# The last output product split around two rows' transposes, the root's table loaded early, the layer norm's transposes one product earlier

## The chip, the cores and the metric

The kernel runs on one core of a Trainium2 chip. The metric is the time of one execution on the device, in microseconds (us). The core has TensorE (PE, the matrix products), VectorE (DVE), ScalarE (ACT), GpSimd (POOL) and SyncE (SP); each works through its own instructions in order, and they wait for each other by semaphores. DMAs are issued here from SP and POOL, and one or two from ACT.

## The reference

One decoder layer on 512 tokens with a model width of 1024, in fp32. Three branches run beside each other, are weighed by gates and merged; an output product and a gated feed-forward part with a short convolution follow:

```python
h = rmsnorm(x) * norm_mix_g
p_a, p_b, q, p_g = split(h @ w_in, [3072, 5120, 6144])          # 9216 columns
gb, gc, v = split(p_a, 3);  y_a = (gb * causal_dwconv3(gc * v)) @ w_a_out
u, ug = split(p_b, 2);      u = causal_dwconv31(u * sigmoid(ug)) + bias
y_b = silu(layernorm(u)) @ w_b_out                              # "branch B"
y_c = attention(q, rmsnorm(mem) @ w_kv) @ w_att_out             # 4 heads, 256 memory tokens
g = sigmoid(p_g + b_gate)
x = x + (g[0] * y_a + g[1] * y_b + g[2] * y_c) @ w_o
u = causal_dwconv3(rmsnorm(x) @ w_up);  gt, up = split(u, 2)    # 2 x 2816 columns
x = x + (silu(gt) * up) @ w_down
return rmsnorm(x) * norm_final_g
```

## The kernel before, in words

**Arithmetic.** Each factor of a product is split into a high and a low part of a format that PE reads faster than fp32, and three matmuls (high by high, high by low, low by high) stand for one. For weights the high part is a copy on ACT (L481, `whi`) and the low part a difference on DVE (L485, `wlo`); activations are split in the same way. Large products are made of blocks by a scheme with seven products in place of eight: a *quad* has products numbered 1, 5, 2, 6, 7, 4, 3, whose operands are sums and differences of activation blocks (`b00`, `b10`, `b11`, `t4` to `t7`, the names in the profile's `fb10h`, `ft4h` and so on) and of weight blocks. Products are summed up in PSUM banks and read out between them: the read of one product frees the bank, or puts away a part result, before the next may go on. The reads of a quad are called r1 to r7; those on ACT are copies (L704 is r6, L712 is r4), those on DVE are additions or subtractions (L438 is r7). One quad product (L662) is 24 matmuls of 256 columns, 128 deep.

**Order.** PE's order is written out by hand. Everything else is a job with an engine, a cost, what must be done before it, and the buffers that it takes or uses. A small planner in the kernel works out from PE's order when each job is due, shifts some kinds of job by a table of constants, plays the engines forward with the jobs' costs, and writes down in which order each engine issues its jobs. The order of ACT, DVE, SP and POOL is therefore made anew when a job is added or PE's order changes. On the chip these orders are fixed: an instruction that waits holds up everything behind it on its engine.

**Around the first two edits' place (about 500 to 546 us).** The last two quads of the input projection are gates ("gate (1,0)" and "gate (1,1)"), with the small products of the merge among them. Meanwhile branch B's layer norm runs: a sum of squares on DVE, its sum over the columns on PE (`pe_squares`), the root on ACT (in `scale_jobs`), the reciprocal on DVE, and then `pe_rows`: four transposes on PE (L800) that spread the factor of each token over all partitions. After them DVE multiplies four blocks by these rows (L1318, `lns`), ACT applies the swish, and ACT and DVE make the operands of branch B's product (L1367, L1372 and others; Y in the planner's words). That product, `mq`, is two quads whose products alternate. The gates' sigmoids are L1492, on ACT. Both sigmoid and swish need a table of their own on ACT, and so does the square root; a change shows as ACT_TABLE_LOAD in the trace.

**Around the other edits' place (about 580 to 612 us).** The merged sum is multiplied by w_o in seven products a, b, f, c, d, e, g, each in two halves (`pe_wo(p, i)`, i the half of the inner dimension; L432 to L434; f alone in single fp32 matmuls). The results are added to or subtracted from x's rows on DVE (L1730, `add_row`). The rows are four blocks of 128 tokens, here called the first to the fourth row (t = 0 to 3); the first two are finished by the products up to e, the other two by g. For each row follow: the square with its sum on ACT (L1737), the root on ACT (L1743), reciprocal and scaling on DVE (L1747, L1748, `xnorm`), eight transposes on PE (L1756, `pe_transpose_rows`), and from the two transposed banks the high parts on ACT (L1768), the low parts on DVE (L1774) and plain copies on ACT (L1781, `h2b`), from which the operands of the up projection are made. The up projection's first products (b00, (up 0, 1) and on) need the first two rows, later ones the other two. Product g writes to banks that the adds of an earlier product must have read. In the kernel before, the first row's transposes stand ahead of g's first half and the second row's between its halves; the third's and fourth's follow in the up projection.

Of the kernel before, what the change touches and what calls it, by code (L numbers as in the profile page):

```python
# [17 lines left out]
SEQ = 512  # L18
NT = SEQ // P
# [297 lines left out]
def hybrid_block_kernel(  # L317
# [19 lines left out]
    nc = tc.nc  # L337
# [27 lines left out]
    job = jobs.add  # L365
# [28 lines left out]
    def dve(n):  # L394
        return (n + 151) / 960.0 - 0.08

    def actv(n):
        return (n + 224) / 1200.0 - 0.08
# [21 lines left out]
    def par(key, i):  # L420
        return pk[:, cols[key] + i : cols[key] + i + 1]
# [23 lines left out]
    def pe(key, cost, fn, after=(), take=(), use=(), unit=True):  # L445
        pe_jobs[key] = (cost, fn, after, take, use)
        seq.append(key)
        if unit:
            the_unit(key, key)

    def the_unit(unit, last):
        unit_at[unit] = len(unit_uses)
        unit_uses.append((unit, last))
# [282 lines left out]
    def column(i, n):  # L736
        return cols_1[:, i : i + n]

    R_MEM, R_X, R_V, SS_X, ATT = column(0, MC), column(2, NT), column(60, NT), 6, 12
# [46 lines left out]
    def squares_to_tokens(bank, key, n, width, total=1024):  # L786

        ps, sq = make(bank), tiles[key]
        for c in range(n):
            for j in range(0, total, width):  # L790
                nc.tensor.matmul(
                    ps[:, c : c + 1], sq[:, j + c * P : j + (c + 1) * P], mean_col,
                    start=j == 0, stop=j + width == total,
                )

    def along_tokens(bank, r, n):

        ps = make(bank)
        for c in range(n):
            nc.tensor.transpose(  # L800
                ps[:, c * P : (c + 1) * P], r[:, c : c + 1].broadcast_to([P, P]), ident
            )
# [205 lines left out]
    def pe_squares(s, key, n, width, after, total=1024):  # L1008
        pe((s, "squares"), n * (total // width) * 0.22,
           lambda: squares_to_tokens(("ss", s), key, n, width, total), after,  # L1010
           take=[(("ss", s), "ps")], use=[key], unit=False)

    def pe_rows(s, r, n):
        pe((s, "rows"), n * 0.11, lambda: along_tokens(("rows", s), r, n), [(s, "scale")],
           take=[(("rows", s), "ps")], unit=False)
# [419 lines left out]
    for p in range(4):  # L1435
# [5 lines left out]
            lambda k, j, p=p: par("conv_a_w", k * KC + 2 * p + j), [("CV", p), ("ldp",)], ANY,  # L1441
# [15 lines left out]
    def merge_product(br, m, g):  # L1457
        w_hi, w_lo = w_units.pop(("merge", br, m, g))
        for j in range(2):
            bank = ("bank", "y", br, m, j)  # L1460
            ps = make(bank) if g == 0 else tiles[bank]
            at = slice(j * P, (j + 1) * P)
            for i in range(4):
                k = 4 * g + i
                hi, lo = (two((s, k // 2))[:, k % 2, :] for s in PARTS[br])
                first, last = k == 0, k == KC - 1
                nc.tensor.matmul(ps, w_hi[:, i, at], hi, start=first, stop=False)  # L1467
                nc.tensor.matmul(ps, w_hi[:, i, at], lo, start=False, stop=False)  # L1468
                nc.tensor.matmul(ps, w_lo[:, i, at], hi, start=False, stop=last)  # L1469

    def pe_merge(br, m, gs=(0, 1)):
        banks = [("bank", "y", br, m, j) for j in range(2)]
        for g in gs:
            parts = [(s, 2 * g + i) for i in range(2) for s in PARTS[br]]
            ready = PARTS_READY[br]
            ready = ready[len(ready) // 2 * g : len(ready) // 2 * (g + 1)]
            pe(("merge", br, m, g), 24 * MM, lambda g=g: merge_product(br, m, g),
               [("wl", ("merge", br, m, g))] + ready,
               take=[(b, "ps") for b in banks] if g == 0 else [],
               use=parts + (banks if g else []))  # L1480

    for br in (2, 0, 1):
        for m in range(4):
# [27 lines left out]
            elif br == 1:  # L1511
# [23 lines left out]
                for r in range(2):  # L1535
                    part = ("mg", r, m // 2)

                    def merged(m=m, gate=gate, r=r, part=part):
                        if m % 2 == 0:
                            make(part)  # L1540
                        at = slice(r * HALF, (r + 1) * HALF)
                        nc.vector.tensor_tensor(
                            four(part)[:, 2 * (m % 2) : 2 * (m % 2) + 2, :],
                            two(("g", 2, m))[:, :, at], two(gate)[:, :, at], op=ALU.add,
                        )
# [45 lines left out]
    def wo_bank(p):  # L1591


        return "a" if p in "aceg" else "f" if p == "d" else p
# [77 lines left out]
    for n, p in enumerate(WO):  # L1672
        if p in "ab":
            m = 0 if p == "a" else 2
# [5 lines left out]
    def wo_lows(p, i):  # L1680
        return ("mgl", p, i) if p in "ab" else ("mgl", p)
# [24 lines left out]
    def pe_wo(p, i):  # L1706

        before = WO_BEFORE.get(p)
        for ts in ((0, 1),) if p in "ab" else ((0,), (1,)):
            banks = [("bank", "wo", wo_bank(p), t) for t in ts]  # L1710
            if p in WO_WHOLE:
                work, cost, needs = wo_whole, 2 * MM_WHOLE, [whole[p, i][1]] + merged(p)
                parts = [SPLIT_FROM[p], whole[p, i][0]]
            else:
                work, cost, needs = wo_product, 6 * MM, [("wl", ("wo", p, i)), wo_lows(p, i)]
                parts = [("mgh", p), ("mgl", p)]
            if i == 0 and before:
                needs += [("x1", before, t) for t in ts]
            new = p not in WO_BEFORE and i == 0
            key = ("wo", p, i) if len(ts) == 2 else ("wo", p, i, ts[0])  # L1720
            pe(key, cost * len(ts), lambda ts=ts: work(p, i, ts), needs,
               take=[(b, "ps") for b in banks] if new else [],
               use=parts + ([] if new else banks), unit=False)
        if (p, i) not in WO_HELD and p not in WO_WHOLE:
            the_unit(("wo", p, i), key)
# [9 lines left out]
    def row_square(t):  # L1735
# [2 lines left out]
            tiles["xnorm", t], tiles["x1", t], AF.Square, accum_out=column(SS_X + t, 1)  # L1738
        )

    def row_root(t):
        r = column(SS_X + t, 1)
        nc.scalar.activation(r, r, AF.Sqrt, bias=eps, scale=1.0 / D)  # L1743
# [48 lines left out]
    for t in range(NT):  # L1792
        both = [("x1", p, t % 2) for p in WO if any(r == t // 2 for r, _, _ in WO_READ[p])]
        job(("keep", t), "SP", 1.6, lambda t=t: nc.sync.dma_start(
            out=x1_kept[t], in_=tiles["x1", t]), both, LOAD_LATENCY, use=[("x1", t)])
        job(("xsquare", t), "ACT", actv(1024), lambda t=t: row_square(t), both,
            take=[(("xnorm", t), "sb")], use=[("x1", t)])
        job(("xroot", t), "ACT", 0.3, lambda t=t: row_root(t), [("xsquare", t)])
        job(("xnorm", t), "DVE", 1.40, lambda t=t: row_norm(t),
            [("xroot", t), "ldg"], use=[("xnorm", t), ("x1", t), ("gffn",)])  # L1800
        for i in range(2):
            bank, r = ("bank", "tr", t, i), t // 2
            if (i, r) != (0, 1):
                job(("rh", t, i), "ACT", actv(512), lambda t=t, i=i: row_high(t, i), [("tr", t)],
                    use=[bank])
                job(("rl", t, i), "DVE", dve(512), lambda t=t, i=i: row_low(t, i), [("rh", t, i)],
                    use=[bank])
                form_ready.setdefault(("h2", f"b{i}{r}"), []).append(("rl", t, i))
            blk = ("h2b", i, r)
            job(("rb", t, i), "ACT", actv(512), lambda t=t, i=i: row_block(t, i), [("tr", t)],  # L1810
                use=[bank] + ([blk] if t % 2 else []), take=[] if t % 2 else [(blk, "lf")])
            blocks_ready[i, r].append(("rb", t, i))

    def pe_transpose_rows(t):
        pe(("tr", t), 0.87, lambda: transpose_rows(t), [("xnorm", t)],
           take=[(("bank", "tr", t, i), "ps") for i in range(2)], use=[("xnorm", t)], unit=False)
# [55 lines left out]
    for do in (  # L1872
# [16 lines left out]
    GATE = {(br, i): ("gate", br, i) for br in range(3) for i in range(2)}  # L1889
# [19 lines left out]
        (GATE[0, 1], 3): lambda: [pe_merge(0, m) for m in range(3)],  # L1909
        (GATE[1, 0], 6): lambda: pe_mean("mu"),  # L1910
        (GATE[1, 1], 6): lambda: (
            pe_squares("v", ("csq", 0), NT, SEQ, [("var", "fold")], SEQ), pe_merge(0, 3, (0,))),
        (GATE[1, 1], 7): lambda: (pe_rows("v", R_V, NT), pe_merge(0, 3, (1,))),
        (GATE[1, 1], 3): lambda: [
            multiply_job(("mq", q), f, "y") for f in (1, 5, 2, 6, 7, 4, 3) for q in range(2)],
    }
# [3 lines left out]
            beside[q, f]()  # L1920

    for p in WO:
        for i in range(2):
            if p == "g":
                pe_transpose_rows(i)
            pe_wo(p, i)


    ENDS = [slice(0, 256), slice(256, 512)]
# [168 lines left out]
    for u, ps in enumerate(PAIR_UNITS):  # L2098
        n = ps.stop - ps.start
        for p in "abe":  # L2100
            i, j = {"a": (0, 0), "b": (1, 0), "e": (1, 1)}[p]
# [217 lines left out]
```

## Time and profile before

| | |
|---|---|
| median of 3 runs | 934.01 us (931.47 to 934.22) |
| the profiled execution | 931.92 us by its time, span 930.2 us from the first to the last instruction |
| mean granted PE clock in it | 0.996 of full speed |
| busy share | PE 98%, PE's weight loads 93%, DVE 91%, ACT 74%, POOL 15% |
| DMA | 196.91 MB, mean 212 GB/s |

How to read the rows that follow: in a row of the timeline the numbers are the start in us from the beginning of the span and the duration; then come engine, line of the kernel, operation, output <- inputs, shapes, and xN for N like instructions in a row. Square brackets give how long the engine stood idle just before, and for whom. In the view of waits a row gives the total, the number and the longest of such waits. In the table by stretches a row is a stretch of time, its length, the busy time of PE, weight loads, DVE, ACT and POOL with the instructions counted, and at the end the granted clock, the busy share of the DMA engines and GB/s.

### The profile page before, as it was taken

What the parts mean: (1) busy time and instruction counts of PE and PEld (TensorE: products, weight loads), DVE (VectorE), ACT (ScalarE), POOL (GpSimd) and SP (SyncE); (2) the same over time, 40 slices, a digit from 0 to 9 for tenths busy, and PEclk for the clock granted to TensorE, in tenths of its full rate; (3) what the DMA queues carried; (4) which work ended last, traced back from release to release, by engine and by line L of the source; (5) the groups of instructions that cost most, each with busy time, mean ns of one, the idle gap of its engine ahead of it and who ended that gap; (6) DMA issues with size and microseconds to landing.
All of it is one profiled execution on the core that took longest, in us unless ns stands there. A gap on an engine that the chain in (4) does not pass through costs nothing.

```text
span 930.2 us, 17118 instructions
## 1 busy us (share of the span) xinstructions
PE 915.1 (98%) x6813; PEld 863.5 (93%) x6813; DVE 848.1 (91%) x976; ACT 686.0 (74%) x938; POOL 137.4 (15%) x165
## 2 busy tenths in 40 slices
PE   9999999999999999999999999999999999999996
PEld 8999999999889999999899897799999999988885
DVE  7998999999989999999886999797999889999986
ACT  8577988889978867878767983686766667765665
POOL 0121111000011111120101211111221111002300
PEclk9999999999999999999999999999999999999999
DMA  9999579745688898887868899889999886689952
GB/s 363 382 251 227 123 182 220 166 114 113 165 183 222 204 203 202 215 187 212 181 140 214 199 252 330 206 211 305 278 245 230 201 167 128 169 313 316 248 110 91
DMA packets 55952, 196.91 MB, mean 212 GB/s; under 512 B 6336, under 2 KB 6464, under 8 KB 55872
## 3 DMA queue, kind: packets, MB, share of 16 engines
q0 software_dynamic: 22608, 81.54, 48.4%
q1 hardware_dynamic: 32544, 113.23, 33.5%
q8 instruction: 53, 0.87, 0.4%
q10 hardware_dynamic: 720, 1.06, 0.3%
q14 instruction: 27, 0.22, 0.1%
HBM read 191.60 MB, written 4.19 MB: 211 GB/s over the span
## 4 chain that ended last, share of the span: by engine, by line
PE 83%; issue 7%; DMA 4%; DVE 3%; ACT 1%; POOL 1%; ACTq 0%; POOLq 0%; DVEq 0%
PE bank L662 55%; PE bank L432 6%; PE bank L434 6%; PE bank L433 5%; PE bank L1469 3%; PE bank L1467 3%; PE bank L1468 3%; PE bank L918 2%; DMA wo<-in_w_o 2%; DMA wf<-in_w_b_out 2%; DMA wf<-in_w_up 1%; DVE wlo L485 1%; ACT whi L481 0%; PE bank L1155 0%; POOL whol L502 0%
## 5 line engine op out<-in xcount | busy, mean ns | idle before, releaser
L481 ACT CAST whi<-wf 128x1024 fp32r<-128x1024 f32 x202 | 210.6, 1045 | 92.4 <-PE bank L662 37.5
L485 DVE TENSOR_TENSOR wlo<-wf,whi 128x1024 fp32r<-128x1024 f32 (+1 forms) x196 | 235.8, 1210 | 23.5 <-ACT whi L481 23.2
L1227 ACT ACTIVATE tp<-u,pk 128x510 f32<-128x510 f32 (+22 forms) x184 | 119.0, 705 | 4.5 <-DVE acc L1234 2.0
L1234 DVE TENSOR_TENSOR acc<-acc,tp 128x988 f32<-128x988 f32 (+22 forms) x92 | 109.0, 1186 | 8.8 <-ACT tp L1227 7.4
L619 POOL DMA_DIRECT2D wf<-in_w_in x48 | 42.9, 908 | 230.7 <-DVE wlo L485 167.4
L662 PE MATMUL bank<-fb10h,whi 128*128 128x256 f32 x248 | 69.0, 278 | 1.7 <-ACT g L712 1.3
L662 PE MATMUL bank<-fb10l,whi 128*128 128x256 f32 x248 | 68.6, 277 | 0.6 <-DVE fb10l L1372 0.6
L662 PE MATMUL bank<-ft6h,whi 128*128 128x256 f32 x248 | 68.7, 277 | 0.1
L662 PE MATMUL bank<-fb11h,wlo 128*128 128x256 f32 x248 | 68.6, 277 | 0.1
L662 PE MATMUL bank<-ft6l,whi 128*128 128x256 f32 x248 | 68.7, 277 | 0.0
L662 PE MATMUL bank<-fb00h,whi 128*128 128x256 f32 x248 | 68.7, 277 | 0.0
L662 PE MATMUL bank<-ft5l,whi 128*128 128x256 f32 x248 | 68.7, 277 | 0.0
L662 PE MATMUL bank<-fb11h,whi 128*128 128x256 f32 x248 | 68.7, 277 | 0.0
L662 PE MATMUL bank<-ft7h,whi 128*128 128x256 f32 x248 | 68.7, 277 | 0.0
L662 PE MATMUL bank<-ft7l,whi 128*128 128x256 f32 x248 | 68.7, 277 | 0.0
L662 PE MATMUL bank<-ft7h,wlo 128*128 128x256 f32 x248 | 68.7, 277 | 0.0
L662 PE MATMUL bank<-fb00l,whi 128*128 128x256 f32 x248 | 68.6, 277 | 0.0
L662 PE MATMUL bank<-fb00h,wlo 128*128 128x256 f32 x248 | 68.6, 277 | 0.0
L662 PE MATMUL bank<-ft6h,wlo 128*128 128x256 f32 x248 | 68.6, 277 | 0.0
L662 PE MATMUL bank<-ft5h,wlo 128*128 128x256 f32 x248 | 68.6, 277 | 0.0
L662 PE MATMUL bank<-ft5h,whi 128*128 128x256 f32 x248 | 68.6, 277 | 0.0
L662 PE MATMUL bank<-fb11l,whi 128*128 128x256 f32 x248 | 68.5, 276 | 0.0
(416 smaller groups left out, 3151.7 us busy)
## 6 DMA issues: line engine op xcount, KB each, us to landing
wf<-in_w_in SPq DMA_DIRECT2D x52, 512.0 KB, 5.1
wf<-in_w_in POOLq DMA_DIRECT2D x48, 512.0 KB, 6.2
wf<-in_w_up POOLq DMA_DIRECT2D x31, 512.0 KB, 7.3
wf<-in_w_up SPq DMA_DIRECT2D x29, 512.0 KB, 7.9
wf<-in_w_down SPq DMA_DIRECT2D x15, 512.0 KB, 4.5
wf<-in_w_att_out SPq DMA_DIRECT2D x8, 512.0 KB, 3.8
wf<-in_w_a_out SPq DMA_DIRECT2D x8, 512.0 KB, 3.7
wf<-in_w_b_out SPq DMA_DIRECT2D x8, 512.0 KB, 6.4
```

The lines of the kernel that those rows point to most:

```text
L432: nc.tensor.matmul(ps, s_hi, w_hi, start=start, stop=False, skip_group_check=again)
L433: nc.tensor.matmul(ps, s_hi, w_lo, start=False, stop=False, skip_group_check=again)
L434: nc.tensor.matmul(ps, s_lo, w_hi, start=False, stop=stop, skip_group_check=again)
L481: nc.scalar.copy(parts[0], src())
L485: nc.vector.tensor_tensor(lo, src(), hi.bitcast(F32), op=ALU.subtract)
L619: nc.gpsimd.dma_start(out=tiles[key], in_=block(w, col[c], k), accum_op=ALU.add)
L662: nc.tensor.matmul(ps[:, c, :], w[:, k, at], a[k], start=first and n == 0, stop=i == 3 and n == 2, skip_group_check=again,)
L1227: nc.scalar.activation(two(("tp", p, s))[:, j, s:], two(("u", p))[:, j, : SEQ - s], AF.Copy, scale=weight(j),)
L1234: nc.vector.tensor_tensor(a, a, two(("tp", p, s))[:, :, s:], op=ALU.add)
L1467: nc.tensor.matmul(ps, w_hi[:, i, at], hi, start=first, stop=False)
L1468: nc.tensor.matmul(ps, w_hi[:, i, at], lo, start=False, stop=False)
L1469: nc.tensor.matmul(ps, w_lo[:, i, at], hi, start=False, stop=last)
```

## The change

Three things are changed. In the last of the output products, g, the order on PE was: first row's transposes, g's first half, second row's transposes, g's second half. It becomes: first half, both rows' transposes, second half. A job "roots" loads the square root's table on ACT by itself, after all twelve sigmoid jobs, and each root of the rows depends on it. And the four transposes of the layer norm's factors (`pe_rows("v", ...)`) move from behind product 7 of the gate quad (1,1) to a place ahead of it, behind half of a merge product.

```diff
@@ -1738,6 +1738,9 @@
             tiles["xnorm", t], tiles["x1", t], AF.Square, accum_out=column(SS_X + t, 1)
         )
 
+    job("roots", "ACT", 1.28, lambda: nc.scalar.preload_act_table_set("sqrt_and_others"),
+        [("sigmoid", br, m) for br in range(3) for m in range(4)])
+
     def row_root(t):
         r = column(SS_X + t, 1)
         nc.scalar.activation(r, r, AF.Sqrt, bias=eps, scale=1.0 / D)
@@ -1795,7 +1798,7 @@
             out=x1_kept[t], in_=tiles["x1", t]), both, LOAD_LATENCY, use=[("x1", t)])
         job(("xsquare", t), "ACT", actv(1024), lambda t=t: row_square(t), both,
             take=[(("xnorm", t), "sb")], use=[("x1", t)])
-        job(("xroot", t), "ACT", 0.3, lambda t=t: row_root(t), [("xsquare", t)])
+        job(("xroot", t), "ACT", 0.3, lambda t=t: row_root(t), [("xsquare", t), "roots"])
         job(("xnorm", t), "DVE", 1.40, lambda t=t: row_norm(t),
             [("xroot", t), "ldg"], use=[("xnorm", t), ("x1", t), ("gffn",)])
         for i in range(2):
@@ -1909,8 +1912,9 @@
         (GATE[0, 1], 3): lambda: [pe_merge(0, m) for m in range(3)],
         (GATE[1, 0], 6): lambda: pe_mean("mu"),
         (GATE[1, 1], 6): lambda: (
-            pe_squares("v", ("csq", 0), NT, SEQ, [("var", "fold")], SEQ), pe_merge(0, 3, (0,))),
-        (GATE[1, 1], 7): lambda: (pe_rows("v", R_V, NT), pe_merge(0, 3, (1,))),
+            pe_squares("v", ("csq", 0), NT, SEQ, [("var", "fold")], SEQ), pe_merge(0, 3, (0,)),
+            pe_rows("v", R_V, NT)),
+        (GATE[1, 1], 7): lambda: pe_merge(0, 3, (1,)),
         (GATE[1, 1], 3): lambda: [
             multiply_job(("mq", q), f, "y") for f in (1, 5, 2, 6, 7, 4, 3) for q in range(2)],
     }
@@ -1920,10 +1924,11 @@
             beside[q, f]()
 
     for p in WO:
-        for i in range(2):
-            if p == "g":
-                pe_transpose_rows(i)
-            pe_wo(p, i)
+        pe_wo(p, 0)
+        if p == "g":
+            for t in range(2):
+                pe_transpose_rows(t)
+        pe_wo(p, 1)
 
 
     ENDS = [slice(0, 256), slice(256, 512)]
```

## The prediction

> **What bounds the kernel now.** First the page's busy times, then who TensorE (PE) waited for, then the granted clock in the stretches where it waited.
>
> ```profile
> PE 915.1 (98%) x6813; PEld 863.5 (93%) x6813; DVE 848.1 (91%) x976; ACT 686.0 (74%) x938; POOL 137.4 (15%) x165
> ```
>
> PE is busy for 915.1 of 930.2 us, and the change removes no product. So it can only win or lose in PE's waits and in stretches where PE runs slowly. The view of waits, for PE alone, names them (us in total, times, longest):
>
> ```profile
> PE bank L662 <- ACT g L712: 1.3, 1, 1.3
> PE bank L1756 <- DVE cols L1747: 1.0, 1, 1.0
> PE bank L662 <- DVE y L438: 1.0, 1, 1.0
> PE bank L432 <- DVE x L1730: 0.8, 1, 0.8
> PE bank L662 <- DVE fb10l L1372: 0.6, 1, 0.6
> PE bank L662 <- ACT fb10h L1367: 0.5, 1, 0.5
> ```
>
> The change touches both places these come from: four waits (L662) lie in the last branch's product at 526 to 546 us, two (L1756, L432) before and after the first transpose of the normed rows. The table by stretches (length; busy us by engine; then the granted clock, DMA share and GB/s) adds a third loss:
>
> ```profile
> 529.80:533.20 3.40, 2.14 (x19) 1.94 (x18) 3.40 (x5) 3.38 (x5) 0.86 (x1) 1.00 0.95 387
> 591.70:595.10 3.40, 1.53 (x11) 0.99 (x10) 3.36 (x5) 3.40 (x5) 0.00 (x0) 1.00 1.04 271
> 595.10:598.50 3.40, 3.40 (x9) 2.63 (x10) 3.40 (x4) 1.25 (x3) 0.00 (x0) 0.50 0.06 13
> ```
>
> After the two waits around the transpose PE runs 3.4 us at half clock, which costs 1.7 us. After the 1.3 us wait in the first row the clock stays at 1.00. So in reach are 1.9 us of waits and 1.7 us of slow clock at 592 to 598, and 3.3 us of waits at 526 to 546.
>
> **Part A: the layer norm's transposes one product earlier.** Moving four transposes ahead of a 2.8 us product costs PE nothing in itself, and the scaling by the norm (L1318) can start 2.4 us sooner (a product less the transposes). But both queues behind it are written in an order that a planner makes, and it comes out anew. Comparing the two programs' orders, one thing matters: on ScalarE (ACT) the read L712, which frees the PSUM bank for the second b10 product, now has ahead of it all that it had before, and two things more: the second half of t4's high part, and one more change of table, because the sigmoids and swishes alternate once more before it.
>
> ```profile
> 532.23 1.28 ACT L1492 ACT_TABLE_LOAD   x1
> 533.52 1.34 ACT L1492 ACTIVATE g<-g,pk 128x512 f32<-128x512 f32 x2
> ...
> 537.70 0.40 ACT L1367 CAST ft4h<-acc 128x256 fp32r<-128x256 f32 x1
> 538.01 0.40 ACT L1367 CAST ft4x<-acc 128x256 fp32r<-128x256 f32 x1
> 538.31 0.57 ACT L704 COPY y<-bank 128x512 f32<-128x512 f32 x1
> ```
>
> Counted from start to start (neighbouring rows overlap by 0.1 us), the load takes 1.29 us and the two casts 0.61, so L712 comes 1.90 us later, because ACT has no gap there to take them in. The earlier norm does not help it: ACT, not the norm, is late. What PE does with that:
>
> ```profile
> 529.78 0.28 PE L662 MATMUL bank<-fb10h,wlo 128*128 128x256 f32 x1
> 531.32 0.38 PE L662 MATMUL bank<-fb10h,whi 128*128 128x256 f32 x1 [1.26 <-ACT g L712]
> ...
> 546.18 0.39 PE L662 MATMUL bank<-ft4h,whi 128*128 128x256 f32 x1 [0.99 <-DVE y L438]
> ```
>
> The product at 531.32 moves to 533.22. The two waits before it (0.5 and 0.6) go, since swish and b10's parts now come before L712; PE then only arrives earlier and stands in one piece for 0.46 + 0.56 + 1.26 + 1.90 = 4.2 us. The later wait of 0.99 is for VectorE's (DVE) subtraction L438, which is not moved by L712: PE comes 1.90 later and waits 0.99 less. Part A costs 1.90 - 0.99 = **0.9 us**. Bounds: nothing if ACT were to gain what the norm gains, 1.9 if L438 is late by as much.
>
> A page of the Trainium skill, ScalarE: Activation LUTs (What ACT_TABLE_LOAD costs), puts a change of set at about 2.66 us, load and drain. Here the next activation starts 1.29 us after the load does, so the trace does not agree and decides; by that figure part A would cost, as an estimate, 1.4 us more.
>
> **Part B: the root's table and the last output product.** The table now loads before the output product, just ahead of a read (L704) whose product has time to spare: after it ACT has this gap.
>
> ```profile
> 542.40 1.05 ACT L481 CAST whi<-wf 128x1024 fp32r<-128x1024 f32 x1 [1.07 <-PE bank L662]
> ```
>
> There I take it as free; without that cover it would cost up to 1.28 us. What it leaves, at 590 us, is on the path:
>
> ```profile
> 586.66 1.05 ACT L481 CAST whi<-wo 128x1024 fp32r<-128x1024 f32 x1 [2.84 <-PE bank L434]
> 587.62 1.05 ACT L1737 ACTIVATE xnorm<-x 128x1024 f32<-128x1024 f32 x1
> 588.57 0.18 ACT L1737 ACTIVATION_READ_ACCUMULATOR xnorm<-x 128x1 f32 x1
> 588.66 1.04 ACT L1737 ACTIVATE xnorm<-x 128x1024 f32<-128x1024 f32 x1
> 589.61 0.18 ACT L1737 ACTIVATION_READ_ACCUMULATOR xnorm<-x 128x1 f32 x1
> 589.81 1.28 ACT L1743 ACT_TABLE_LOAD   x1
> 591.11 0.48 ACT L1743 ACTIVATE cols<-cols,eps 128x1 f32<-128x1 f32 x2
> ```
>
> ```profile
> 593.03 1.28 DVE L1748 SCALAR_TENSOR_TENSOR xnorm<-x,cols,gffn 128x1024 f32<-128x1024 f32 x1
> 594.23 1.28 DVE L1730 TENSOR_TENSOR x<-x,bank 128x512 f32<-128x512 f32 x2
> ```
>
> ```profile
> 591.64 0.39 PE L434 MATMUL bank<-whi,mgl 128*128 128x512 f32 x1
> 593.06 1.06 PE L1756 MATMUL bank<-ident,xnorm 128*128 128x128 f32 x8 [1.03 <-DVE cols L1747]
> 594.96 0.67 PE L432 MATMUL bank<-whi,mgh 128*128 128x512 f32 x1 [0.84 <-DVE x L1730]
> ...
> 599.42 1.04 PE L1756 MATMUL bank<-ident,xnorm 128*128 128x128 f32 x8
> 600.21 0.48 PE L432 MATMUL bank<-whi,mgh 128*128 128x512 f32 x1
> ...
> 603.02 0.28 PE L662 MATMUL bank<-fb00h,whi 128*128 128x256 f32 x1
> ```
>
> Product e ends at 592.03 (593.06 - 1.03). Product g needs the adds L1730, which in both programs stand on DVE behind both normed rows. So g must wait for the whole chain in either order; new is only that the transposes no longer stand between. The squares are pinned by the weights that arrive at 586.6, so without the load the chain is 1.30 us earlier: adds at 592.93, g at 593.66. By part A e ends 0.9 later, at 592.96: PE stands 0.7 us. Then a half of g (600.21 to 603.02: 2.81), both rows' transposes (0.79 each, 599.42 to 600.21), the other half: 593.66 + 2.81 + 1.58 + 2.81 = 600.86, against 603.02. That is **-2.2 us**, part A's 0.9 counted in, if the clock holds.
>
> **Part C: what the bunched transposes make late.** After them ACT has four casts and four copies in one go, ahead of the next row's square; in the trace they come in two groups, the first under the slow product. On DVE the difference for (up 0, 5) now stands ahead of the third row's norm, which it did not.
>
> ```profile
> 599.62 1.05 ACT L481 CAST whi<-wf 128x1024 fp32r<-128x1024 f32 x1 [3.26 <-PE bank L434]
> 600.57 0.58 ACT L1768 CAST fb00h<-bank 128x512 fp32r<-128x512 f32 x1
> ...
> 604.67 1.06 ACT L1737 ACTIVATE xnorm<-x 128x1024 f32<-128x1024 f32 x1 [0.39 <-DVE x L1730]
> ```
>
> ```profile
> 602.16 0.69 DVE L1774 TENSOR_TENSOR fb00l<-bank,fb00h 128x512 fp32r<-128x512 f32 x1 [0.24 <-ACT h2b L1781]
> ...
> 604.56 1.22 DVE L485 TENSOR_TENSOR wlo<-wf,whi 128x1024 fp32r<-128x1024 f32 x1
> ...
> 606.48 1.29 DVE L1748 SCALAR_TENSOR_TENSOR xnorm<-x,cols,gffn 128x1024 f32<-128x1024 f32 x1
> ```
>
> The 0.24 shows that the readers of one transposed bank on ACT and DVE wait for each other; in the new order it is the copies that wait for the differences. From the end of g's first half: 0.2 until its result is out, a high part 0.97, four casts 2.0 (3.2 so far); meanwhile DVE does a difference of 1.14 and four of 0.60, the third done at 4.3; the last three copies follow it (5.9), a high part (6.9), the square and its sum (7.9), the high part of (up 0, 5) (8.9), its difference on DVE (10.1), reciprocal and norm (11.6). PE has until then 1.58 + 2.81 and two products of 2.83 (603.02 to 605.85, and up to 608.68), 10.05. So it waits **1.6 us** for the third row; in the trace it does not wait there. Bounds: 1.0 if the copies don't wait for the differences, 1.9 if the (up 0, 5) weights are late.
>
> **The sum.** The profiled execution took 931.92 us by its time, with a span of 930.2. Without a fall of the clock: -2.2 + 1.6 = -0.6, so 931.3. Does it fall? In the trace it fell when no product ran from 592.03 to 594.96, 2.9 us, and did not after 1.26. Part A's gap is 4.2 us, longer than the one that lost the clock; B's is 0.7, C's 1.6 with 0.79 of transposes behind it. So I expect one fall, in A: 1.7 us. Part of that comes back. PE then ends e at 594.66; the second square waits for d's add and g starts at about 595.0, 1.34 later than without the fall and not 1.7. So +0.8 instead of -0.6: 932.7.
>
> The runs' median, 934.01, lies 2.1 above the profiled execution, and the trace doesn't show why (another fall would be 1.7). I put half of it, 1.0, on the forecast: **933.7 us**, -0.3 against the median, +1.8 against the profiled one. That is no change, as 0.3% (2.8 us) is about what a measurement of this kernel can tell.
>
> **Rivals.** *The clock holds in A.* The third loss goes entirely: 931.3, or 932.3 with the 1.0. For it: 1.26 us and then 0.99 us of waiting left the clock at 1.00. Against it: the gap is three times as long. The Trainium skill, TensorE: Matmul & The Clock Gate (Part 1: The HAM clock gate), has the clock halve after at least one idle window of some 3.4 us, free-running. Taken strictly, a 4.2 us gap holds a whole window in about one case of four, an estimate from its figure, and this rival would be the likeliest; the trace, where a gap of 2.9 us with transposes in it was enough, doesn't agree with so strict a reading, and I weigh it a little below the forecast.
>
> *The clock falls again in C* (slower): with the transposes PE has no product for 1.6 + 0.79 = 2.4 us there, near the 2.9 that lost it. Then 1.7 more, paid in full: 934.4 in the frame of the profiled execution, 936.5 with the full 2.1, and with the upper ends of A and C (1.0 and 0.3) 937.8. It decides from a gap of about 2.4 us on.
>
> *The change doesn't do what it says in A*: if L712 is not delayed, because ACT gains the norm's lead, A gains up to 0.9 and the gap stays under 2.9: about 930.4, or 931.4 with the 1.0.
>
> **Numbers.** Chances: forecast 0.42, clock holds 0.25, a second fall 0.23, A not as said 0.10. Faster by over 0.3% means below 931.2: a third of the clock that holds (0.08) and seven tenths of the last (0.07), 0.15. Slower means above 936.8: two thirds of the second fall (0.15) and a fifth of the forecast, its upper ends (0.08), 0.23. Within: 0.62. The range goes from 930.4 (A not as said, in the frame of the profiled execution) to 937.8 (the second fall with its upper ends), and little of either case lies outside.
>
> **What would show it.** Of the profile after: one PE wait of about 4 us for L712 in place of three, no wait for L438; at g one wait of about 0.7 for L1730 and none at L1756 there; a wait of 1 to 2 us at the third row's transposes (L1756). No table load between squares and roots. One stretch of half clock behind the first of these, none at 595. Wrong would be: no wait at the third row, a long wait for L712 missing, or table loads in a new place that PE waits for.

## The result, and the profile after

The changed kernel takes 935.13 us (median of 14 runs, 933.71 to 935.80), the kernel before 931.88 (14 runs, 931.04 to 934.22). The ratio, estimated over all these runs, is 1.0030 with a 95% interval of 1.0023 to 1.0037, that is 2.8 us; the medians lie 3.25 us apart. The profiled execution of the changed kernel took 934.44 us with a span of 932.7, against 931.92 and 930.2: 2.5 us.

The page's busy times and the view of waits for PE, kernel after (L1759 and L1750 are L1756 and L1747 of the kernel before):

```profile
PE 916.5 (98%) x6813; PEld 866.2 (93%) x6813; DVE 848.9 (91%) x976; ACT 686.5 (74%) x938; POOL 137.1 (15%) x165
```

```profile
PE bank L662 <- ACT g L712: 4.6, 1, 4.6
...
PE bank L1759 <- DVE cols L1750: 1.3, 1, 1.3
PE bank L432 <- DVE x L1730: 0.7, 1, 0.7
```

The three short waits of the first place and the one at L438 are gone; one wait of 4.6 us for L712 stands there. Before g there is only the wait for the adds, 0.7 us, and the third row's transposes wait 1.3 us. These are the waits that the prediction named (4.2, 0.7 and 1.6), though the 0.7 agrees by luck: with the fall of the clock its own sum had PE there at 594.66 and g at 595.0, a wait of 0.3. The chain of ScalarE shows why L712 is late, as foretold: one table load more (five from 500 us on, not four) and two more casts of t4 ahead of it, together 2.0 us, and no idle time in either kernel.

```profile
525.59 1.28 ACT L1492 ACT_TABLE_LOAD   x1
526.89 1.34 ACT L1492 ACTIVATE g<-g,pk 128x512 f32<-128x512 f32 x2
...
531.49 0.93 ACT L1367 CAST ft4h<-acc 128x512 fp32r<-128x512 f32 x2
...
533.10 0.60 ACT L712 ACTIVATE g<-bank 128x512 f32<-128x512 f32 x1
```

The clock, in the table by stretches cut at the times at which it changes:

```profile
529.15:532.56 3.41, 0.02 (x1) 0.00 (x0) 3.31 (x4) 3.41 (x7) 0.00 (x0) 1.00 0.94 336
532.56:535.97 3.41, 2.22 (x10) 2.22 (x11) 3.41 (x7) 3.41 (x7) 0.86 (x1) 0.50 1.04 297
535.97:539.39 3.42, 3.42 (x18) 3.42 (x17) 3.42 (x5) 2.19 (x4) 1.75 (x2) 0.50 0.93 175
539.39:542.80 3.41, 3.41 (x32) 3.41 (x31) 2.66 (x5) 2.67 (x4) 0.00 (x0) 1.00 1.03 180
```

PE works 0.02 us in the first stretch, and the clock is half in the next two: the fall lasts 6.8 us, two windows, not one. In the second PE works 2.22 of 3.41 us and the clock does not come back. At 595 there is no fall any more.

Where the time goes is seen from the starts of the same PE work in both traces (the rows that the prediction doesn't show stand below, of before and then of after):

| PE work | before | after | later by |
|---|---|---|---|
| product b00 of the last gate | 514.74 | 515.17 | 0.43 |
| second b10 product, after the wait for L712 | 531.32 | 533.75 | 2.43 |
| first t4 product of the last branch | 546.18 | 550.10 | 3.92 |
| g's first half | 594.96 | 596.48 | 1.52 |
| the up projection's first product | 603.02 | 603.86 | 0.84 |
| the third row's transposes | 608.68 | 611.00 | 2.32 |
| span | 930.2 | 932.7 | 2.5 |

```profile
514.74 0.28 PE L662 MATMUL bank<-fb00h,whi 128*128 128x256 f32 x1
...
608.68 1.03 PE L1756 MATMUL bank<-ident,xnorm 128*128 128x128 f32 x8
```

```profile
515.17 0.28 PE L662 MATMUL bank<-fb00h,whi 128*128 128x256 f32 x1
...
533.75 0.58 PE L662 MATMUL bank<-fb10h,whi 128*128 128x256 f32 x1 [4.58 <-ACT g L712]
...
550.10 0.28 PE L662 MATMUL bank<-ft4h,whi 128*128 128x256 f32 x1
...
596.48 0.51 PE L432 MATMUL bank<-whi,mgh 128*128 128x512 f32 x1 [0.68 <-DVE x L1730]
599.38 1.91 PE L1759 MATMUL bank<-ident,xnorm 128*128 128x128 f32 x16
...
603.86 0.28 PE L662 MATMUL bank<-fb00h,whi 128*128 128x256 f32 x1
...
611.00 1.06 PE L1759 MATMUL bank<-ident,xnorm 128*128 128x128 f32 x8 [1.33 <-DVE cols L1750]
```

The first 0.43 stands in work that the change doesn't touch, and it arises within the first 15 us; in the traces of the experiments it lies between 0.3 and 1.6, and times of two traces differ by that much from the start. Without it the changed kernel is 2.0 later behind L712 (1.9 was forecast), 3.5 later at 546 (forecast 0.9 and 1.7), 1.1 later at g (forecast: at the same time, 595.0) and 0.4 later at the up projection (forecast: 0.8 earlier). That is where the sum went wrong, and the weights show how:

```profile
589.59 1.05 ACT L481 CAST whi<-wo 128x1024 fp32r<-128x1024 f32 x1 [2.75 <-DMA wo<-in_w_o]
590.54 1.06 ACT L1737 ACTIVATE xnorm<-x 128x1024 f32<-128x1024 f32 x1
...
591.59 1.04 ACT L1737 ACTIVATE xnorm<-x 128x1024 f32<-128x1024 f32 x1
...
592.63 0.46 ACT L1746 ACTIVATE cols<-cols,eps 128x1 f32<-128x1 f32 x2
```

The table load between squares and roots is gone, and the roots follow 1.04 us behind the second square. But the cast ahead of the squares, which had started at 586.66, starts at 589.59. (The row of before names a product of PE as the release. By the trace's record of landings the weights came at 586.58, 0.01 us ahead of that product's release, so either alone would have held the cast.) GpSimd issues these weights as the last of three loads in a row, and the first of the three (L1614) waits for VectorE's low part of an earlier block of w_o. The rows of before, and then of after:

```profile
568.54 1.22 DVE L485 TENSOR_TENSOR wlo<-wo,whi 128x1024 fp32r<-128x1024 f32 x1
...
570.05 0.86 POOL L1614 DMA_DIRECT2D wo<-in_w_o  x1 [12.31 <-DVE wlo L485]
570.59 2.11 POOL L1607 DMA_DIRECT2D wo<-in_w_o  x2
```

```profile
570.86 1.22 DVE L485 TENSOR_TENSOR wlo<-wo,whi 128x1024 fp32r<-128x1024 f32 x1
...
572.38 0.86 POOL L1614 DMA_DIRECT2D wo<-in_w_o  x1 [10.54 <-DVE wlo L485]
572.91 2.11 POOL L1607 DMA_DIRECT2D wo<-in_w_o  x2
```

Of the two L1607 the second is the one that counts; it is issued at 571.13 and at 573.45, 2.3 us later, and lands at 586.58 and at 589.51, 2.9 us later. VectorE, in turn, reaches the low part 2.3 us later, behind the work of branch B and the merge, and has next to no room to catch up. The table by stretches, before and then after (fourth number: VectorE):

```profile
520.00:530.00 10.00, 8.98 (x75) 8.45 (x74) 8.41 (x12) 9.97 (x15) 1.76 (x2) 1.00 1.01 229
530.00:545.00 15.00, 13.74 (x121) 13.67 (x120) 13.94 (x19) 13.20 (x19) 2.62 (x3) 1.00 1.02 280
545.00:565.00 20.00, 19.01 (x132) 17.33 (x131) 19.96 (x30) 10.92 (x14) 3.46 (x4) 1.00 0.96 250
```

```profile
520.00:530.00 10.00, 9.17 (x79) 8.84 (x78) 7.06 (x11) 9.95 (x14) 2.47 (x3) 1.00 0.91 170
530.00:545.00 15.00, 11.25 (x75) 11.25 (x76) 13.70 (x19) 11.85 (x19) 2.62 (x3) 0.77 0.99 249
545.00:565.00 20.00, 20.00 (x160) 19.27 (x159) 19.63 (x29) 14.26 (x17) 3.45 (x4) 1.00 0.99 248
```

From 520 to 530 us VectorE works 7.06 us instead of 8.41 (ScalarE, busy in both for all of the 10 us, feeds it later), and from 545 to 565 it works 19.63 of 20 us: what it loses it does not make up. Over the 45 us it does 1.9 us less, which with the 0.43 of the start agrees with the 2.3 by which the low part is late. The DMA engines' share is 0.99 in the last two of these stretches, and the transfer, issued 2.3 us later, does not make it up either.

### The profile page after: what moved, and what is told of

Read it like the earlier page. It is cut to its first block, busy times and chain, and to the rows that moved or that the text cites. A ratio compares the mean times of both kernels' runs of the same rounds, so it can differ in the third digit from the quotient of the medians.

```text
span 932.7 us, 17111 instructions
## 1 busy us (share of the span) xinstructions
PE 916.5 (98%) x6813; PEld 866.2 (93%) x6813; DVE 848.9 (91%) x976; ACT 686.5 (74%) x938; POOL 137.1 (15%) x165
## 3 DMA queue, kind: packets, MB, share of 16 engines
q10 hardware_dynamic: 720, 1.06, 0.3%
## 4 chain that ended last, share of the span: by engine, by line
PE 84%; issue 7%; DMA 3%; DVE 2%; ACT 2%; POOL 1%; ACTq 0%; POOLq 0%
PE bank L662 56%; PE bank L434 5%; PE bank L432 5%; PE bank L433 5%; PE bank L1469 3%; PE bank L1467 3%; PE bank L1468 3%; PE bank L918 2%; DMA wo<-in_w_o 2%; DMA wf<-in_w_b_out 1%; ACT whi L481 1%; DVE wlo L485 1%; DVE xnorm L1751 0%; PE bank L1155 0%; POOL whol L502 0%
## 5 line engine op out<-in xcount | busy, mean ns | idle before, releaser
L481 ACT CAST whi<-wf 128x1024 fp32r<-128x1024 f32 x202 | 210.7, 1045 | 92.9 <-PE bank L662 40.2
L485 DVE TENSOR_TENSOR wlo<-wf,whi 128x1024 fp32r<-128x1024 f32 (+1 forms) x196 | 236.3, 1213 | 22.5 <-ACT whi L481 22.3
L662 PE MATMUL bank<-fb10h,wlo 128*128 128x256 f32 x248 | 69.9, 282 | 0.0
```

Of the source, the lines that this page charges most:

```text
L481: nc.scalar.copy(parts[0], src())
L485: nc.vector.tensor_tensor(lo, src(), hi.bitcast(F32), op=ALU.subtract)
L662: nc.tensor.matmul(ps[:, c, :], w[:, k, at], a[k], start=first and n == 0, stop=i == 3 and n == 2, skip_group_check=again,)
```

## The experiments

The theory after this result: (1) the early table is a gain; (2) the earlier transposes of the layer norm make L712 late, and this costs through VectorE and the w_o weights; (3) the split of g is a loss of its own. The rivals: all of the loss is (2) or all of it is (3); and, for (2), that it is the half clock that costs. Each run is compared with runs of the kernel before on the same chip, 931.84 to 931.99 us.

**Each part alone.** Only the early table:

```diff
+    job("roots", "ACT", 1.28, lambda: nc.scalar.preload_act_table_set("sqrt_and_others"),
+        [("sigmoid", br, m) for br in range(3) for m in range(4)])
...
-        job(("xroot", t), "ACT", 0.3, lambda t=t: row_root(t), [("xsquare", t)])
+        job(("xroot", t), "ACT", 0.3, lambda t=t: row_root(t), [("xsquare", t), "roots"])
```

> Only the early load of the root's table, nothing else changed. Theory (three parts with prices of their own: the early table gains, the other two lose): the chain square, root, norm, add is 1.3 us shorter, so the gap before g falls from 2.9 to about 1.6 us and the clock does not fall there, which gives 1.3 + 1.7 = 3.0 us: about 929 us. If the clock falls in spite of the shorter gap: about 930.5. Rival (the load was hidden, or its new place costs what the old one did): no change, 931.9, or up to 933 if the read behind the load makes TensorE wait.

Measured 930.36 us (11 runs, 929.01 to 932.11), ratio 0.9984 (0.9975 to 0.9994): 1.5 us faster. The trace bears out the mechanism. PE's rows around g, with the early table alone:

```profile
592.50 1.03 PE L1759 MATMUL bank<-ident,xnorm 128*128 128x128 f32 x8
593.41 0.50 PE L432 MATMUL bank<-whi,mgh 128*128 128x512 f32 x1
593.75 0.40 PE L433 MATMUL bank<-wlo,mgh 128*128 128x512 f32 x1
```

g starts at 593.41 instead of 594.96, at the full clock (0.34 and 0.24 from start to start, where the kernel before had 0.43), and at 613 us PE is 3.0 us ahead, as expected. PE waits 0.6 us for the read L704 behind the load, but no longer the 1.0 us for L438. At the end it is 2.2 us ahead in this trace (928.0 against 930.2): 0.9 is given back between 613 and 680 us, in waits too small to name. In the medians it is 1.5 us. The size was off, not the sign.

A part of the 3.0 was probably never there in most runs. In all traces here the clock falls behind PE's last product, which takes 0.0016 to 0.0032 off the mean clock; a fall of 3.41 us at 595 takes 0.0018 more. The profiled execution of before has 0.996. Of the 54 runs of before beside the experiments 27 have 0.998 or more, which leaves no room for that fall, 25 have 0.997, which hardly does, and two have less. Without the fall the early table can win the 1.3 us of the load and not the 1.7 of the clock. This is read from mean clocks alone, as only one run of before has a trace.

Only the split of g:

```diff
-        for i in range(2):
-            if p == "g":
-                pe_transpose_rows(i)
-            pe_wo(p, i)
+        pe_wo(p, 0)
+        if p == "g":
+            for t in range(2):
+                pe_transpose_rows(t)
+        pe_wo(p, 1)
```

> Only g's two halves around both rows' transposes. Theory: the gap before g stays 2.9 us, now without the first row's transposes in it, so these 0.8 us come on top, and the clock falls there as in the kernel before; the third row's transposes wait 1.3 to 1.7 us. Together 2.1 to 2.5 us slower: about 934.2. Rival (the split is a gain and the whole loss of the change is the earlier layer-norm transposes): 931 or less.

Measured 934.95 us (5 runs), ratio 1.0037 (1.0024 to 1.0049): 3.1 us slower. The waits of PE are the ones of the theory:

```profile
PE bank L432 <- DVE x L1730: 2.7, 1, 2.7
...
PE bank L1756 <- DVE cols L1747: 1.3, 1, 1.3
```

g waits 2.7 us in one piece; in the kernel before the same stretch held the first row's transposes. The size, 3.1 us, is above the 2.1 to 2.5 of the theory. The rival, that the split is a gain, is refuted.

Only the layer norm's transposes:

```diff
-            pe_squares("v", ("csq", 0), NT, SEQ, [("var", "fold")], SEQ), pe_merge(0, 3, (0,))),
-        (GATE[1, 1], 7): lambda: (pe_rows("v", R_V, NT), pe_merge(0, 3, (1,))),
+            pe_squares("v", ("csq", 0), NT, SEQ, [("var", "fold")], SEQ), pe_merge(0, 3, (0,)),
+            pe_rows("v", R_V, NT)),
+        (GATE[1, 1], 7): lambda: pe_merge(0, 3, (1,)),
```

> Only the layer norm's four transposes one product earlier. Theory: ScalarE's read L712 comes 2.0 us later, TensorE stands 4.6 us in one piece, and the clock falls there for two windows of 3.4 us, of which TensorE loses 2.6; 1.0 us comes back at L438. That is 3.6 us later at 546 us; about one of it, up to 1.7 if the clock no longer falls before g, comes back there: 933.8 to 935.5 us, a middle of 934.6. Rival (the loss is all in the split order of g): 931.9.

Measured 934.45 us (11 runs, 932.71 to 934.97), ratio 1.0026 (1.0018 to 1.0035): 2.6 us slower, as expected, and with the 4.6 us wait for L712. So neither rival stands: both edits lose, 2.6 and 3.1, the early table gains 1.5; together 4.2, where the whole change measured 3.25.

**The split inside the change.** The changed kernel with g's old order (the split's diff above, undone):

> The changed kernel with the old order of g (first row's transposes, half, second row's, half): what the split costs inside the change. Theory: the split puts the first row's transposes, which the wait for the adds covered, on the path, and bunches the casts so that the third row waits 1.3 us: without it 2.0 to 2.2 us less than the changed kernel, about 933.0, no wait of over 0.3 us at the third row. Rival (with the early table the split costs nothing any more): 935.1.

Measured 932.78 us (11 runs), ratio to before 1.0007 (0.9998 to 1.0016), that is 2.35 less than the changed kernel, and the third row does not wait. The early table and the earlier transposes together are thus no change that can be told from none, and the split makes up 2.35 of the 3.25.

**Does the half clock cost?** The changed kernel, with the product ahead of the long wait computed twice, so that PE works in it:

```diff
-        for c in range(2):
+        for c in ((0, 1) * 2 if (q, f) == (("mq", 0), 2) else range(2)):
```

> The changed kernel; the product that stands ahead of the 4.6 us wait is computed twice (the second time over the first), so TensorE works 2.8 us of that wait and the rest of the wait is 1.8 us; all waits and orders stay as they are. Theory (the clock falls because no product runs, and the half clock costs 2.6 us): no fall in 530 to 540, some 0.4 us given back at g, so 2.2 us faster than the changed kernel: about 932.9. Rival (the loss is the wait alone, the slow stretch is hidden by what is late anyway): 935.1 as the changed kernel, or 0 to 3 more if the added matmuls are on the path.

Measured 934.33 us (6 runs, 933.45 to 937.00), ratio to before 1.0032 (1.0020 to 1.0043). In the profiled execution the clock fell again, for one window. The table by stretches:

```profile
532.02:535.43 3.41, 1.53 (x13) 1.37 (x12) 3.41 (x6) 3.41 (x7) 0.86 (x1) 1.00 0.87 306
535.43:538.85 3.42, 3.42 (x18) 3.42 (x17) 3.42 (x5) 3.29 (x6) 1.75 (x2) 0.50 0.91 183
```

A wait of 1.9 us that fell into one window of 3.41 left PE 1.53 us of work, and the clock fell. Three of the six runs have a mean clock of 0.998, as high as where it does not fall (below); they took 934.02, 934.64 and 934.75 us, the other three 933.45, 933.97 and 937.00. So 36 matmuls were repeated instead of 24:

```diff
-        for c in range(2):
+        for c in ((0, 0, 1, 0, 1) if (q, f) == (("mq", 0), 2) else range(2)):
```

> The changed kernel with 36 matmuls repeated ahead of the 4.6 us wait instead of 24 (a half of the product and then the product, each written over by the next pass), so that TensorE works 4.2 us of it and stands only 0.4 to 0.5. With 24 the wait was still 1.9 us and the clock fell for one window instead of two. Theory (the clock falls when TensorE works less than about half of a 3.4 us window, and the two slow windows cost 2.6 us): no fall in 530 to 540; 2.6 us won at 546, of which 0.3 to 0.5 us go to a longer wait for the adds before g: 2.2 us faster than the changed kernel, about 932.9, and 1.4 faster than with 24 repeated. Rival (the fall has another cause than the idle time, such as the load of the arrays or the phase of the runs): a slow stretch there as before, 934 to 935.

Measured 935.87 us (5 runs, 935.18 to 936.91), ratio to before 1.0043 (1.0029 to 1.0056). The clock does not fall (its mean is 0.998): that part of the theory holds, and the rival of this run, another cause of the fall, is refuted. At 549 us PE is 1.9 us earlier than in the changed kernel, but the time is not better. In the view of waits and on ScalarE it reads:

```profile
PE bank L432 <- DVE x L1730: 1.7, 1, 1.7
```

```profile
589.40 1.05 ACT L481 CAST whi<-wo 128x1024 fp32r<-128x1024 f32 x1 [3.65 <-DMA wo<-in_w_o]
```

The w_o weights come at 589.40 as they did at 589.59, and g starts at 596.29, 0.2 us earlier, after a wait of 1.7 instead of 0.7. VectorE's low part ahead of their issue comes 0.6 us earlier (570.23), so does the issue (572.81), and the weights land 0.2 earlier. Between 640 and 660 us PE then falls behind the changed kernel by 1.4, with waits for VectorE of 0.25 and 0.54 us.

So of what the half clock takes at 546, little reached g here: a PE that is faster there meets VectorE and the DMAs. The price of 2.2 us fell in both runs (24 repeated matmuls gave 0.8 us, 36 took 0.7). That the half clock costs nothing is not shown. In the two kernels with g's old order and the earlier transposes, the runs with the higher mean clock were the faster ones, as far as so few tell: without the early table 932.71 and 933.57 us at 0.996 against 933.62 to 934.97 at 0.994, with it a median of 932.40 at 0.996 against 933.03 at 0.994 and 0.995.

**Is it the order of DMA issues?** In the changed kernel a w_o load stands behind a load of the last branch that waits for its buffer; before it stood ahead. The exchange of these two alone, in the changed kernel and in the one with 36 repeated matmuls:

```diff
+HELD, BEHIND, LATE = ("ld", (("mq", 1), "r")), ("ld", ("wo", "y", 0)), []
...
-            fn()
+            LATE.append(fn) if key == HELD else (fn(), key == BEHIND and LATE.pop()())
```

> The changed kernel with two DMA issues on SyncE in the order of the kernel before: the load of a w_o block (for the fourth row of output blocks) ahead of the last quad's load, which waits some 5 us for its buffer. Nothing else moves. Theory (in the changed kernel the w_o load stands behind an issue that waits; the DMA engines, full from 526 to 612 us, don't catch up, and the last w_o weights reach ScalarE 2.5 us later, which sets the squares and g): the w_o load issues 4 to 5 us earlier, the cast of the last-but-one w_o weights ahead of the squares comes 1 to 2.5 us earlier than 589.6, and g, which TensorE reaches late anyway, gains the 0.7 us that it waited: about 934.4. Rival (the weights are late because the DMAs are full and the buffers free late, whatever the order): no change, 935.1.

> The same exchange of two DMA issues in the kernel with 36 matmuls repeated, where the clock doesn't fall, TensorE is 2.1 us earlier at 549 us than in the changed kernel, and all of it is lost at g, which waits 1.7 us for the adds. Theory (the late w_o weights took the gain): the weights before the squares arrive 1 to 2.5 us earlier, the wait for the adds before g falls from 1.7 to under 0.7 us, 1 to 2 us faster than without the exchange: 934 to 935. Rival (the DMAs are full and nothing is gained by order): the wait stays 1.7 us, 935.9.

Measured 934.49 us (7 runs, 934.19 to 935.66), ratio to before 1.0030 (1.0020 to 1.0041), and 935.54 (5 runs, 934.62 to 935.87), 1.0035 (1.0021 to 1.0049). Against 935.13 and 935.87 that is 0.6 and 0.3, inside the spread. The w_o load is issued some 4 us earlier, at about 528 instead of 532.12, but the cast of the weights ahead of the squares starts at 589.35 in the first (589.59 without the exchange) and at 590.85 in the second (589.40). At 515 us the first trace lies 1.2 us behind that of the changed kernel, but its clock falls for one window and not two, which gives about as much back. So neither shows a gain by the order of these two issues. The load that sets the squares is another one, issued by GpSimd behind VectorE; to free VectorE alone was not tried.

**Is it the table loads?** The changed kernel with two sigmoids of the last gate held back, by their due times in the planner (lines shift by 4 in this kernel and the next: L716 is L712, L485 is L481):

```diff
+KEY_LATER = {("sigmoid", 1, 1): 33, ("sigmoid", 1, 2): 30}
...
+        for key, d in KEY_LATER.items():
+            due[key] += d
         return due, users
```

> The changed kernel with two of the sigmoids of the last gate (the second and third) held back on ScalarE until the swishes are done: two changes of table fewer ahead of L712, everything else as the planner makes it from that. Theory (L712 is late because of table loads that the changed order alternates): the 4.6 us wait goes, and with it the slow clock; L438 may wait up to 1.7 us instead. Without the 2.6 us of slow clock and with 2.9 us less waiting: 5.5 us less than the changed kernel, about 929.6. Rival (L712 is late because of its place behind other reads and casts, not of the loads): the wait stays over 3 us and the time above 933.

Measured 930.88 us (11 runs, 929.60 to 932.35), ratio to before 0.9990 (0.9982 to 0.9999): 4.25 us less than the changed kernel. On ScalarE:

```profile
529.30 0.61 ACT L716 ACTIVATE g<-bank 128x512 f32<-128x512 f32 x1
```

```profile
585.64 1.05 ACT L485 CAST whi<-wo 128x1024 fp32r<-128x1024 f32 x1 [2.82 <-DMA wo<-in_w_o]
```

L716 comes 3.8 us earlier than in the changed kernel: between 500 us and it there are two table loads instead of five. The loads are not all of it: four sigmoid activations (2.5 us) and a part of the t4 casts, too, now stand behind it, and 2.8 us of idle time ahead of it, so this run shows the order on ScalarE as the cause and does not part the loads from the sigmoids. The wait of 4.6 us is gone (L438, here L442, is waited for 1.5 us, as allowed for), the w_o weights come 3.95 us earlier, and g starts at 593.05, 3.4 earlier. Together with the 36 repeated matmuls, where PE was early and the weights were not, this says what g follows: the weights, not PE.

**Without the waits.** What the runs point to: the early table alone, the sigmoids held back, and L712 given an earlier due time.

```diff
+KEY_LATER = {("sigmoid", 1, 1): 27, ("sigmoid", 1, 2): 27, ("r4", ("gate", 1, 1)): -5}
```

> The kernel before with the early table alone, and two shifts of due times in the planner: the second and third sigmoid of the last gate later (27 us), the read L712 earlier (5 us). Theory (what makes TensorE wait at 526 to 541 us is ScalarE, which changes tables twice more than it must; what makes it wait before g is the table load): none of the waits over 0.5 us between 520 and 610 us is left and no slow clock there: 3.4 us of waits less than with the early table alone (930.4), 926.5 to 927.5. Rival (VectorE or the DMAs are the next limit right behind): 929 to 930.5.

Measured 928.40 us (5 runs, 927.88 to 929.80), ratio 0.9962 (0.9950 to 0.9975): 3.6 us faster than before, and the fastest of all. It lies between the theory and its rival. None of the waits that it was to remove is left; the longest of PE behind the start are now

```profile
PE bank L437 <- DMA whol<-in_w_o: 1.1, 2, 0.6
PE bank L666 <- DVE wlo L489: 0.6, 1, 0.6
```

so the DMAs and VectorE take back a part, as the rival said.

## Why the prediction was wrong

The forecast was 933.7 us, no change; measured were 935.13, 3.25 us more than before.

- **Part A, the delay**: right. L712 came 2.0 us later (1.90 forecast), the waits merged into one of 4.6 (4.2), and the wait for L438 went.
- **The clock**: a fall was foretold there, and none at g, and both came. Its length was mis-sized: two windows, not one, about 2.5 us at 546 instead of 1.7. What of it reaches the end is open: with no fall there (36 repeated matmuls) g started only 0.2 us earlier and the kernel was no faster.
- **Part B, the step that failed**: "the squares are pinned by the weights that arrive at 586.6, so without the load the chain is 1.30 us earlier: adds at 592.93, g at 593.66". The chain did lose the load, which was free in its new place (at 540.13, with 0.73 us of idle time behind it). Its start was not pinned: the weights are issued behind work of VectorE that the branch delayed by part A makes late, and the cast came 2.5 us later (589.59 less the 0.43 of the start). 2.5 less 1.3 is 1.2, and g started 1.1 later than before. The fall that was put behind it (g at 595.0) hid half of this error, by luck. From g on the two traces run as the sum says: its miss at the end, 1.3 us in the profiled executions, is the 1.1 at g.
- **Part C**: right, and by the mechanism named: a copy on ScalarE waits 0.61 us for a difference on VectorE. The third row waited 1.3 us (1.6 forecast, bounds 1.0 to 1.9).
- **The frame**: the sum stood at +0.8 against the profiled execution, and then half of 2.1 us, by which the median of three runs lay above that execution, was added to the forecast; the result was compared with the full median. Of the 14 runs of before the median is 931.88, and the profiled execution's 931.92 was a typical time. Its clock was not, by the means of the other runs: the fall at 595, whose end the sum counts as a gain of 1.7, seems to be missing in most of them. In its frame the forecast was 932.7; measured were 934.44 in the profiled execution.
- **The rivals**: the clock that holds and A not as said did not happen. Of the second fall the sign was right (slower) and its place was not: in the third row's window PE worked enough, and the clock stayed at 1.00.

What stays open: what the half clock at 533 us costs at the end, where the early table's gain goes behind 613 us, and whether VectorE or the full DMA engines alone would hold the w_o weights back.

## What to carry to other kernels

A time in the trace at which data arrive is itself the end of a chain: before a sum holds it fixed, follow it back to what let its transfer start, and ask whether the change moves that. Where VectorE and the DMAs are as full as TensorE, a faster clock or an earlier product on TensorE alone may buy little (here 1.9 us at 549 became 0.2 at g). Transposes that fill a wait are free where they stand: moved out of it they are on the path. A fall of the clock in one profiled execution need not be in the others: compare the mean clocks of all runs before it is put into a sum. Three runs are too few to correct a forecast by the distance of their median from the profiled execution.

## What the runs showed of the hardware

In each trace the clock changes at times that lie a whole number of 3.41 us apart (in the kernel before 4.63 and 595.13 us, 173 such windows), and it does not need a whole window without products to fall. In the windows of 3.41 us that end where it fell, PE's busy time was 0.02 us (after), 1.53 (24 repeated matmuls) and 1.54 (before, 1.06 of it transposes, 591.72 to 595.13); it held after windows with

```profile
592.83:596.25 3.42, 1.72 (x8) 1.09 (x6) 3.35 (x6) 2.92 (x4) 0.86 (x1) 1.00 1.04 316
```

1.72 us (36 repeated matmuls). In all twelve traces no full-clock window of 1.72 us or more ended in a fall. So the limit lies near a half of a window, between 1.53 and 1.72 us here (two windows without transposes), and what counts is how a wait lies over the windows: 1.9 us within one lost the clock, and the kernel before keeps it over 2.3 us of waits (0.46, 0.56, 1.26) that are spread over three windows. To come back it needs more than the fall does: with 2.22 us of work in a slow window (after) it stayed slow, and with 2.71 (the earlier transposes alone) too. With 3.05 it came back at the end of that window (after with the two DMA issues exchanged). The two rows, in this order:

```profile
533.52:536.93 3.41, 2.71 (x12) 2.71 (x13) 3.41 (x7) 3.41 (x7) 0.86 (x1) 0.50 0.93 293
```

```profile
534.57:537.98 3.41, 3.05 (x14) 3.05 (x15) 3.41 (x7) 3.41 (x6) 0.67 (x2) 0.50 1.00 286
```

The Trainium skill, TensorE: Matmul & The Clock Gate (Part 1: The HAM clock gate), gives at least one idle window for the fall and one busy window for the return. The second agrees with these rows; the first is too strict, as a window with 1.53 us of products was idle enough. By that rule the clock would have held in the kernel with 24 repeated matmuls, and it did not.
